# A trunk layer whose instruction order a planner writes: the heads' transposes, scores and values placed further behind their operands except for the last heads, and selects counted longer

## The chip, the core and the metric

The kernel runs on one core of a Trainium2 chip. The core has TensorE (PE, with its weight loads shown apart as PEld), VectorE (DVE), ScalarE (ACT), GpSimd (POOL) and a queue that issues DMAs (SP). Each engine works through its own list of instructions in the order in which the program was built, and waits on semaphores for the others. The metric is the device time of one execution in microseconds, the median of several runs; lower is better. Before the change it is 942.58 us (three runs, 942.47 to 942.61).

## What is computed

One layer over 512 tokens of 2048 channels, all in float32:

```
h    = rms_norm(x, norm_g)
proj = h @ w_in                  # 2048 x 8192: qA kA vA gA | qB kB vB gB
# A: 8 heads of 128, stick-breaking attention, strictly causal
z = qA @ kA.T * scale
log_stay = where(causal, log_sigmoid(-z), 0)
after = reversed_cumsum(log_stay) - log_stay
w = where(causal, exp(log_sigmoid(z) + after), 0);  ya = w @ vA
# B: 8 heads of 128, rms-normed q and k, bias by distance, softmax
scores = qB @ kB.T * scale + bias;  yb = softmax(scores) @ vB
out = x + concat(ya * silu(gA), yb * silu(gB)) @ w_out
```

## The kernel before

**The products.** The input projection is cut into 32 units of 256 output channels, in groups of four (query, key, value, gate of two heads); four further units are the output projection. A unit takes four steps, each with 512 KB of weights, and most units use a Winograd scheme of seven block products per step. To keep float32 accuracy every product is three matmuls (`three`, L530 to L532): high part by high part, low by high, high by low. The high part of the weights is a cast on ACT (`wh`, L384), the low part a difference on DVE (`wl`, L388); both are double buffered, and a cast into a buffer waits until PE has used it up.

**The heads.** While PE works on the products of later units, the heads of finished groups are handled piecewise in between. For an A head, `score` issues the score matmuls of four query blocks (b = 0 to 3; three matmuls each, into one of three spare banks); `score_a` then runs Abs, Exp and Ln on ACT (L967 to L969), a causal select on POOL (L962), Relu on ACT (L971), a second select, a scan (L974) and a subtraction (L977) on DVE, which frees the bank, a third select, and an Exp on ACT (L980). `turn` transposes the weights on PE (L1107) and splits them (L1115, L1116). `v_turn` transposes the values (L1138), scales them on ACT (L1144) and splits them; `values` multiplies them. B heads go through `prep_b` (two more transposes, L1008) and `score_b` instead, where a softmax on ACT ends in L1091. Heads are numbered 0 to 15; heads 0, 1, 4, 5, 8, 9, 12 and 13 are A heads.

**What sets the order.** A planner runs while the program is built. Every piece of work is a generator that yields an `Op` with an engine and a duration that the planner counts for it (`DV`, `AC`, `G` for POOL, `M` for PE). The planner keeps a clock of its own; when an engine is free by that clock, it takes from the engine's ready list the operation that is due first. An operation comes onto the ready list some time after its predecessor's planned end (`wait` in `advance`, L174): 0.4 us for PE, 0.06 us for the others. PE's own list goes first, and with nothing on it PE gets the next block of products (`next_product`), which is two triples of matmuls in units 2 to 31. So the numbers decide only where an instruction stands in the list of its engine; on the chip each waits for its real operands.

`position[0]` counts the blocks of products issued so far, and `at_step[step_of[NU - 4, 0]]` is the first block of unit 28, the first of the last group.

Of the kernel before, what the change touches and what calls it, by code (L numbers as in the profile page):

```python
# [26 lines left out]
NEG_BIG = -1e30  # L27
# [5 lines left out]
NU = 4 * NG  # L33
# [30 lines left out]
def trunk_kernel(ctx: ExitStack, tc: tile.TileContext, xT, xn, wi, wqk, wo, ng, qg, kg, rel, out):  # L64
# [34 lines left out]
    def tmp(shape, tag, name, dt=F32, bufs=1):  # L99
        return wp.tile(shape, dt, tag=tag, name=name, bufs=bufs)  # L100
# [33 lines left out]
    def later(t, fn):  # L134
        count[0] += 1
        heapq.heappush(events, (t, count[0], fn))
# [12 lines left out]
    def DV(w, fn, due=None, n=1):  # L149
        return Op("DVE", (0.075 + 1.04e-3 * w) * n, fn, due)  # L150

    def AC(w, fn, due=None, n=1):
        return Op("ACT", (0.085 + 0.85e-3 * w) * n, fn, due)

    def STT(w, fn, due=None):
        return Op("DVE", 0.13 + 1.04e-3 * w, fn, due)

    def M(cost, fn):
        return Op("PE", cost, fn, 0.0)

    def G(cost, fn, due=None):
        return Op("POOL", cost, fn, due)
# [5 lines left out]
    def advance(gen, rank):  # L168
        r = next(gen, None)
        if r is None:  # L170
            return
        if isinstance(r, Op):

            wait = 0.4 if r.engine == "PE" else 0.06  # L174
            later(clock[0] + wait, lambda: ready[r.engine].append((r, gen, rank, count[0])))
        else:
            waiting.append((rank, r, gen))

    def spawn(gen, rank=(0,)):
        advance(gen, rank)  # L180
# [10 lines left out]
    def schedule(next_product):  # L191

        while True:
            while True:

                go_on = False
                for w in sorted(waiting, key=lambda w: w[0]):
                    if w in waiting and w[1]():
                        waiting.remove(w)
                        advance(w[2], w[0])  # L200
                        go_on = True
                if not go_on:
                    break
            for e in ready:
                if busy[e] > clock[0] + 1e-9:
                    continue
                if ready[e]:
                    k = min(ready[e], key=lambda k: (k[0].due(), k[3]))
                    if clock[0] < held[e] - 1e-9 and k[0].due() > clock[0] + 1.5:
                        continue  # L210
                    ready[e].remove(k)
                    op, gen, rank, _ = k
                    end = issue(e, op)
                    later(end, lambda gen=gen, rank=rank: advance(gen, rank))
                    later(busy[e], lambda: None)
                    if op.hold:
                        held[e] = busy[e] + 0.2
                        later(held[e], lambda: None)
                elif e == "PE":
                    op = next_product()  # L220
                    if op is not None:
                        later(issue(e, op), op.after)
                        later(busy[e], lambda: None)
# [30 lines left out]
    at_step = {}  # L254
# [47 lines left out]
    step_of = {s_: n for n, s_ in enumerate(steps_)}  # L302
# [6 lines left out]
    position = [0]  # L309
# [240 lines left out]
    for k in reversed(range(len(program))):  # L550
        n, x, a = program[k]
# [337 lines left out]
    def take(who):  # L889

        yield lambda: len(owner) < len(SPARE)
        i = next(i for i in SPARE if i not in owner)
        owner[i] = who
        return i

    def give(i):
        del owner[i]
# [8 lines left out]
    def drop(tag, i):  # L906
        live[tag][i] = False

    def head(g, h):
        return 2 * g + h  # L910
# [29 lines left out]
    def score(g, h):  # L940

        n = head(g, h)
        yield lambda: all(("prep", n, k) in done for k in range(2)) and (n == 0 or ("scores", n - 1) in done)
        for b in range(NT):
            i = None
            if g % 2 == 0:
                i, = yield from buffer("L")
            else:
                yield lambda: n in bias
            k, = yield from buffer("W")  # L950
            z_ = yield from take(("score", n, b))
            w = P * (b + 1)
            L = tmp([P, S], "L", "L")[:, :w] if g % 2 == 0 else None
            W = tmp([P, S], "W", "W", bufs=3)[:, :w]
            yield M(0.05 + 0.35 * max(256, w) / 256, lambda: scores(banks[:, z_, :], n, b))
            z = banks[:, z_, :w]
            spawn(score_a(n, b, z_, z, L, W, w, i, k) if g % 2 == 0 else score_b(n, b, z_, z, W, w, k), (n, 1))
        done.add(("scores", n))

    def causal(x, fill):  # L960

        pool.affine_select(out=x, in_=x, compare_op=ALU.is_gt, fill=fill, base=0, pattern=[[-1, P]], channel_multiplier=1)  # L962

    def score_a(n, b, z_, z, L, W, w, i, k):
        d = slice(w - P, w)
        q_ = rstds[:, b:b + 1]
        yield AC(w, lambda: act.activation(L, z, AF.Abs, scale=q_))  # L967
        yield AC(w, lambda: act.activation(L, L, AF.Exp, scale=-1.0))
        yield AC(w, lambda: act.activation(L, L, AF.Ln, bias=1.0))  # L969
        spawn(causal_log(n, b, L[:, d]), (n, 1))  # L970
        yield AC(w, lambda: act.activation(W, z, AF.Relu, scale=q_))  # L971
        yield G(0.35, lambda: causal(W[:, d], 0.0))
        yield lambda: ("log", n, b) in done
        yield Op("DVE", 0.08 + 2.1e-3 * w, lambda: dve.tensor_tensor_scan(  # L974
            out=W[:, ::-1], data0=L[:, ::-1], data1=W[:, ::-1], initial=0.0, op0=ALU.add, op1=ALU.add))
        drop("L", i)
        yield STT(w, lambda: dve.scalar_tensor_tensor(out=W, in0=z, scalar=q_, in1=W, op0=ALU.mult, op1=ALU.subtract))  # L977
        give(z_)
        yield G(0.35, lambda: causal(W[:, d], NEG_BIG))
        yield AC(w, lambda: act.activation(W, W, AF.Exp))  # L980
        spawn(turn(n, b, W, k), (n, 2))

    def causal_log(n, b, x):
        yield G(0.35, lambda: causal(x, 0.0))
        done.add(("log", n, b))


# [107 lines left out]
    def turn(n, b, src, k):  # L1095

        yield lambda: ("turn", n, b - 1) in done if b else ("values", n - 1) in done if n else all(("staged", j, 0) in done for j in range(NJ))
        i = yield from take(("turn", n, b))
        if b == 0:
            wT[n] = [tmp([P, 13, P], x, x, F32R) for x in ("wth", "wtl")]  # L1100
            spawn(zeros(n), (n, 2))
        th, tl = wT[n]
        t = banks[:, i, :]

        def fn():
            for j in range(b + 1):
                pe.transpose(t[:, j * P:(j + 1) * P], src[:, j * P:(j + 1) * P], ident)  # L1107

        yield M(0.13 * (b + 1), fn)
        done.add(("turn", n, b))  # L1110
        drop("W", k)
        w = (b + 1) * P
        tv = t[:, :w].rearrange("p (a c) -> p a c", c=P)
        blocks = slice(b, b + 3 * b + 1, 3)
        yield AC(w, lambda: act.copy(th[:, blocks, :], tv))  # L1115
        yield DV(w, lambda: dve.tensor_tensor(out=tl[:, blocks, :], in0=tv, in1=th[:, blocks, :].bitcast(F32), op=ALU.subtract))  # L1116
        give(i)
        done.add(("turned", n, b))
# [9 lines left out]
    def v_turn(g, h):  # L1128
        n = head(g, h)
        yield lambda: "R" in done and ("unit", 4 * g + 2) in done  # L1130
        yield lambda: ("values", n - 1) in done if n else all(("staged", j, 0) in done for j in range(NJ))
        i = yield from take(("v", g, h))
        f = C[g, 2][:, h, :]
        b = banks[:, i, :]

        def fn():
            for t in range(NT):
                pe.transpose(b[:, t * P:(t + 1) * P], f[:, t * P:(t + 1) * P], ident)  # L1138

        yield M(0.5, fn)  # L1140

        def scaled():
            for t in range(NT):
                act.activation(f[:, t * P:(t + 1) * P], b[:, t * P:(t + 1) * P], AF.Copy, scale=rstd[:, t:t + 1])  # L1144

        yield Op("ACT", 0.8, scaled)
        give(i)
        d = vv[n] = tmp([P, 2, S], "v", "v", F32R)
        yield AC(512, lambda: act.copy(d[:, 0, :], f))
        yield DV(512, lambda: dve.tensor_tensor(out=d[:, 1, :], in0=f, in1=d[:, 0, :].bitcast(F32), op=ALU.subtract))  # L1150
        done.add(("v read", n))
        done.add(("v", g, h))
# [134 lines left out]
```

## Time and profile before

| | |
|---|---|
| median of three runs | 942.58 us |
| the profiled execution's own time | 941.64 us |
| its span, from the first instruction to the last | 939.9 us |
| mean granted TensorE clock | 0.998 |
| issued matmuls | 7344 |
| selects on POOL (L962) | 96, 63.8 us busy |

The span is 1.7 us shorter than the execution's own time, and the execution 0.9 us shorter than the median of the runs. In the views, "idle before" is time for which an engine did nothing ahead of an instruction, with the instruction that ended it. PEld is the loading of a matmul's stationary operand, which runs ahead of the matmul while the one before still streams.

### The profile page before, as it was taken

To read this page: it belongs to the slowest core of one execution; us is meant where nothing else is said; L and a number is where in the kernel's file an instruction comes from. 1 tells how busy PE (TensorE), PEld (TensorE's weight loads), DVE (VectorE), ACT (ScalarE), POOL (GpSimd) and SP (SyncE) were. 2 spreads that over 40 slices of the span, in tenths; PEclk is the share of its full clock that TensorE was granted. 3 is DMA by queue.
4 is the path that set the end of the run, shared out by engine and by line. 5 is a ranking of instruction groups with operands and counts; after the bars stand their busy time and mean duration, and the time that the engine had idled before them with its cause. 6 is when DMAs were issued, how large, how long until landed. Compare 5 with 4: busy or idle time off the path is not lost.

```text
span 939.9 us, 19289 instructions
## 1 busy us (share of the span) xinstructions
PE 925.2 (98%) x7344; PEld 903.5 (96%) x7344; DVE 826.1 (88%) x1562; ACT 604.2 (64%) x1150; POOL 82.2 (9%) x157
## 2 busy tenths in 40 slices
PE   9999999999999999999999999999999999999997
PEld 6899999999999999999999999999999999999997
DVE  8999998988898989888989898889989988778785
ACT  7776876884578557845785588457759785534332
POOL 0001220000122000001220000002300000101010
PEclk9999999999999999999999999999999999999999
DMA  8762223233322332233223322332222445556371
GB/s 271 237 208 91 92 91 100 82 105 105 104 91 79 120 106 82 92 110 112 85 78 122 112 80 90 113 111 74 97 91 90 147 153 182 141 199 191 112 191 45
DMA packets 63916, 112.41 MB, mean 120 GB/s; under 512 B 7248, under 2 KB 11856, under 8 KB 63824
## 3 DMA queue, kind: packets, MB, share of 16 engines
q1 hardware_dynamic: 61680, 107.51, 35.1%
q0 software_dynamic: 1728, 3.15, 2.0%
q8 instruction: 57, 0.93, 0.4%
q10 hardware_dynamic: 416, 0.52, 0.2%
q14 instruction: 35, 0.29, 0.1%
HBM read 102.77 MB, written 8.39 MB: 118 GB/s over the span
## 4 chain that ended last, share of the span: by engine, by line
PE 59%; issue 27%; DVE 7%; ACT 3%; POOL 2%; DMA 1%; POOLq 0%; SPq 0%; DVEq 0%; ACTq 0%
PE banks L530 19%; PE banks L531 18%; PE banks L532 18%; DVE wl L388 2%; POOL W L962 2%; PE banks L1107 1%; PE banks L1008 1%; DMA wt<-in_wi 1%; ACT wh L384 1%; DVE W L977 1%; DVE U L722 0%; DVE W L974 0%; DVE wt L362 0%; ACT c L1144 0%; PE banks L1138 0%
## 5 line engine op out<-in xcount | busy, mean ns | idle before, releaser
L530 PE MATMUL banks<-xh,wh 128*128 128x256 f32 (+1 forms) x1744 | 508.1, 291 | 0.1
L532 PE MATMUL banks<-xh,wl 128*128 128x256 f32 (+1 forms) x1744 | 500.3, 287 | 0.3 <-DVE wl L388 0.2
L531 PE MATMUL banks<-xl,wh 128*128 128x256 f32 (+1 forms) x1744 | 500.0, 287 | 0.0
L384 ACT CAST wh<-wt 128x1024 fp32r<-128x1024 f32 (+3 forms) x308 | 286.5, 938 | 237.3 <-PE banks L531 144.0
L388 DVE TENSOR_TENSOR wl<-wt,wh 128x768 fp32r<-128x768 f32 (+3 forms) x308 | 332.4, 1081 | 67.8 <-ACT wh L384 64.6
L530 PEld LDWEIGHTS banks<-xh,wh 128*128 128x128 f32 x1744 | 334.0, 192 | 4.2 <-ACT xh L520 0.7
L532 PEld LDWEIGHTS banks<-xh,wl 128*128 128x128 f32 x1744 | 333.6, 191 | 4.0 <-DVE wl L388 1.6
L531 PEld LDWEIGHTS banks<-xl,wh 128*128 128x128 f32 x1744 | 333.9, 191 | 3.3 <-DVE xl L521 0.3
L531 PE MATMUL banks<-wl,xh 128*128 128x256 f32 x432 | 122.3, 283 | 0.0
L532 PE MATMUL banks<-wh,xl 128*128 128x256 f32 x432 | 122.3, 283 | 0.0
L530 PE MATMUL banks<-wh,xh 128*128 128x256 f32 x432 | 122.2, 283 | 0.0
L362 DVE TENSOR_TENSOR wt<-wt 128x512 f32<-128x512 f32 x144 | 99.4, 690 | 6.1 <-DMA wt<-in_wo 4.8
L530 PEld LDWEIGHTS banks<-wh,xh 128*128 128x128 f32 x432 | 82.9, 192 | 0.0
L531 PEld LDWEIGHTS banks<-wl,xh 128*128 128x128 f32 x432 | 82.9, 192 | 0.0
L532 PEld LDWEIGHTS banks<-wh,xl 128*128 128x128 f32 x432 | 82.9, 192 | 0.0
L366 DVE TENSOR_TENSOR wt<-wt 128x256 f32<-128x256 f32 x144 | 60.5, 420 | 2.5
L365 DVE TENSOR_TENSOR wt<-wt 128x256 f32<-128x256 f32 x144 | 60.6, 421 | 2.1
L962 POOL TENSOR_SCALAR_AFFINE_SELECT W<-W 128x128 f32<-128x128 f32 x64 | 44.1, 689 | 94.5 <-DVE W L977 74.9
L962 POOL TENSOR_SCALAR_AFFINE_SELECT L<-L 128x128 f32<-128x128 f32 x32 | 19.7, 615 | 284.7 <-ACT L L969 278.1
L705 ACT COPY U<-banks 128x512 f32<-128x512 f32 x36 | 21.0, 584 | 25.0 <-PE banks L532 25.0
L1107 PE MATMUL banks<-ident,W 128*128 128x128 f32 x160 | 29.2, 281 | 3.8 <-ACT W L1091 2.4
L1116 DVE TENSOR_TENSOR wtl<-banks,wth 128x128 fp32r<-128x128 f32 (+1 forms) x64 | 30.9, 482 | 0.3 <-ACT wth L1115 0.2
(166 smaller groups left out, 1023.6 us busy)
## 6 DMA issues: line engine op xcount, KB each, us to landing
wt<-in_wi SPq DMA_DIRECT2D x254, 256.0 KB, 2.9
wt<-in_wo SPq DMA_DIRECT2D x64, 256.0 KB, 3.2
xs<-in_xn SPq DMA_DIRECT2D x16, 256.0 KB, 4.1
mixd<-c SPq DMA_DIRECT2D x16, 256.0 KB, 2.0
out<-co SPq DMA_DIRECT2D x16, 256.0 KB, 6.0
x<-in_xT SPq DMA_DIRECT2D x14, 256.0 KB, 4.3
co<-in_xn POOLq DMA_DIRECT2D x12, 256.0 KB, 6.3
bias<-in_rel SPq DMA_DIRECT2D x8, 256.0 KB, 3.4
```

The source lines that it names most:

```text
L362: yield DV(512, lambda: dve.tensor_tensor(out=some(t, 8, -7, 2), in0=some(t, 5, -5, 2), in1=some(t, 1, 0, 2), op=ALU.add), need(k0, 4))
L365: yield DV(256, lambda: dve.tensor_tensor(out=some(t, 9, 2), in0=some(t, 8, 2), in1=some(t, 0, 2), op=ALU.add), need(k1, 4))
L366: yield DV(256, lambda: dve.tensor_tensor(out=some(t, 12, 1), in0=some(t, 9, 2), in1=some(t, 4, 2), op=ALU.add), need(k1, 3.5))
L384: act.copy(whl[n, part][0][:, c], t)
L388: yield DV(c.stop - c.start, lambda: dve.tensor_tensor(out=l[:, c], in0=t, in1=h[:, c].bitcast(F32), op=ALU.subtract), need(k, 0.5))
L530: pe.matmul(o, lh, rh, start=start, stop=False, **kw)
L531: pe.matmul(o, lh, rl, start=False, stop=False, **kw)
L532: pe.matmul(o, ll, rh, start=False, stop=stop, **kw)
L705: act.copy(x[0], pair(u, a, 0, 1))
L962: pool.affine_select(out=x, in_=x, compare_op=ALU.is_gt, fill=fill, base=0, pattern=[[-1, P]], channel_multiplier=1)
L1107: pe.transpose(t[:, j * P:(j + 1) * P], src[:, j * P:(j + 1) * P], ident)
L1116: yield DV(w, lambda: dve.tensor_tensor(out=tl[:, blocks, :], in0=tv, in1=th[:, blocks, :].bitcast(F32), op=ALU.subtract))
```

## The change

The wait of 0.4 us for PE becomes 1.4 us as long as the planner has not reached unit 28, and stays 0.4 us from there on. It holds for every PE operation that a generator yields: transposes, scores and values. Products are not affected directly, as they come from `next_product`. A select is counted with 0.6 us instead of 0.35 us, and the scaling of the values in `v_turn` with 1.25 us instead of 0.8 us. No instruction is added or removed.

```diff
         if isinstance(r, Op):
-            wait = 0.4 if r.engine == "PE" else 0.06
+            wait = 0.06 if r.engine != "PE" else 1.4 if position[0] < at_step[step_of[NU - 4, 0]] else 0.4
             later(clock[0] + wait, lambda: ready[r.engine].append((r, gen, rank, count[0])))
...
-        yield G(0.35, lambda: causal(W[:, d], 0.0))
+        yield G(0.6, lambda: causal(W[:, d], 0.0))
...
-        yield G(0.35, lambda: causal(W[:, d], NEG_BIG))
+        yield G(0.6, lambda: causal(W[:, d], NEG_BIG))
...
-        yield G(0.35, lambda: causal(x, 0.0))
+        yield G(0.6, lambda: causal(x, 0.0))
...
-        yield Op("ACT", 0.8, scaled)
+        yield Op("ACT", 1.25, scaled)
```

What this does to the lists of the engines is shown at three places.

**PE, head 4: from the score of its first block to that block's transpose.** `qk4` are the split queries and keys of the head, `xh` and `wh` the split activations and weights of the products, `W` the block's attention weights. Before:

```order
L530 MATMUL banks_80<-qk4_2859 128x256
L531 MATMUL banks_80<-qk4_2859 128x256
L532 MATMUL banks_80<-qk4_2859 128x256
...
L530 MATMUL banks_80<-xh5_238,wh0_42_3074 128x256
L531 MATMUL banks_80<-xl5_239,wh0_42_3074 128x256
L532 MATMUL banks_80<-xh5_238,wl0_42_3075 128x256
L1107 MATMUL banks_80<-ident_68,W_3141 128x128
```

The same place in the changed kernel:

```order
L530 MATMUL banks_80<-qk4_2818 128x256
L531 MATMUL banks_80<-qk4_2818 128x256
L532 MATMUL banks_80<-qk4_2818 128x256
...
L530 MATMUL banks_80<-xh7_348,wh0_43_3136 128x256
L531 MATMUL banks_80<-xl7_349,wh0_43_3136 128x256
L532 MATMUL banks_80<-xh7_348,wl0_43_3137 128x256
L1107 MATMUL banks_80<-ident_68,W_3140 128x128
```

Before, 45 matmuls of products lie between the score and the transpose; now 63 do, and the transpose stands in weight step 43 instead of 42.

**PE, head 1: from the transpose of its last block to its values.** `wth` and `wtl` are the split transposed attention weights, `v` the split values. Before:

```order
L1107 MATMUL banks_80<-ident_68,W_1638 128x128 x4
L530 MATMUL banks_80<-xh0_118,wh0_24_1704 128x256
...
L531 MATMUL banks_80<-xl1_122,wh1_24_1731 128x256
L532 MATMUL banks_80<-xh1_121,wl1_24_1732 128x256
L530 MATMUL banks_80<-wth_1555,v_1627 128x512
```

In the changed kernel:

```order
L1107 MATMUL banks_80<-ident_68,W_1712 128x128 x4
L530 MATMUL banks_80<-xh4_203,wh0_26_1822 128x256
...
L532 MATMUL banks_80<-xh5_238,wl1_26_1851 128x256
L1008 MATMUL banks_80<-ident_68,c5_1764 128x128 x4
L530 MATMUL banks_80<-wth_1573,v_1642 128x512
```

Before, 24 matmuls of products lie between; now 30 do, and four transposes of the next head besides. The whole place has moved from step 24 to step 26.

**ACT, head 5: its second block.** The 128x128 rows are block 0, the 128x256 rows block 1; `wh` is a cast of product weights. Before:

```order
L967 ACTIVATE L_3553<-banks_80,rstds_76 128x256
L980 ACTIVATE W_3499<-W_3499 128x128
L968 ACTIVATE L_3553<-L_3553 128x256
L384 CAST wh1_48_3580<-wt48_3394 128x768
L969 ACTIVATE L_3553<-L_3553 128x256
L971 ACTIVATE W_3554<-banks_80,rstds_76 128x256
```

In the changed kernel:

```order
L980 ACTIVATE W_3539<-W_3539 128x128
L967 ACTIVATE L_3621<-banks_80,rstds_76 128x256
L968 ACTIVATE L_3621<-L_3621 128x256
L969 ACTIVATE L_3621<-L_3621 128x256
L971 ACTIVATE W_3622<-banks_80,rstds_76 128x256
L384 CAST wh0_50_3694<-wt50_3522 128x1024
```

The Exp of block 0 (L980), which waits for a select on POOL, and a cast of weights stood inside the chain of block 1; now the one stands ahead of it and the other behind it.

The last 1455 rows of PE, from the middle of head 15 to the end of the program, read alike in both kernels.

## Prediction

> **What bounds the kernel now.** I read the page first, then TensorE instruction by instruction, then the waits of its weight loads.
>
> ```profile
> span 939.9 us, 19289 instructions
> PE 925.2 (98%) x7344; PEld 903.5 (96%) x7344; DVE 826.1 (88%) x1562; ACT 604.2 (64%) x1150; POOL 82.2 (9%) x157
> PEclk9999999999999999999999999999999999999999
> ```
>
> PE is busy nearly all the time and its granted clock is full in every slice, so the end is set by how many matmuls there are, at which cadence, and by what PE loses between them. The change leaves the matmuls alone; it can only touch the losses. How a loss looks is seen at the first transpose of head 7, in the timeline of PE and of its loads (start, length, what):
>
> ```profile
> 381.31 0.28 PE L531 MATMUL banks<-xl,wh 128*128 128x256 f32 x1
> 381.43 0.28 PE L532 MATMUL banks<-xh,wl 128*128 128x256 f32 x1
> 382.19 0.33 PE L1107 MATMUL banks<-ident,W 128*128 128x128 f32 x1 [0.48 <-ACT W L1091]
> ...
> 382.19 0.14 PEld L1107 LDWEIGHTS banks<-ident,W 128*128 128x128 f32 x1 [0.69 <-ACT W L1091]
> ```
>
> Products start every 0.12 us. Here 0.76 us pass between two starts, so 0.64 us are lost, although the matmul row counts 0.48 us idle (its matmuls are drawn 0.28 us long, more than twice the cadence). The row of the load says 0.69, close to the true loss. I therefore add up the waits of the loads, over the whole span (total us, times, longest):
>
> ```profile
> PEld banks L1107 <- ACT W L1091: 4.3, 9, 0.7
> PEld banks L1107 <- ACT W L980: 2.8, 8, 0.4
> PEld banks L530 <- DVE W L977: 2.7, 3, 0.9
> PEld banks L530 <- DVE wtl L1116: 1.0, 1, 1.0
> PEld banks L1107 <- ACT c L1144: 0.5, 2, 0.3
> PEld banks L1107 <- DVE wtl L1116: 0.4, 2, 0.2
> PEld banks L530 <- DVE st L1083: 0.3, 1, 0.3
> PEld banks L1138 <- DVE R L880: 0.3, 1, 0.3
> PEld banks L531 <- DVE qk L929: 0.3, 1, 0.3
> PEld banks L532 <- DVE v L1150: 0.3, 1, 0.3
> PEld banks L530 <- DVE qk L1056: 0.2, 1, 0.2
> PEld banks L531 <- DVE wtl L1116: 0.2, 1, 0.2
> ```
>
> All twelve rows are work of the heads: 31 waits, **13.3 us** together, 1.4% of the span. That is the most that the change can win by them. The loads of products wait for a split of weights three times, the last time at 12.89 us, before the change begins:
>
> ```profile
> PEld banks L532 <- DVE wl L388: 1.6, 3, 0.6
> 12.89 0.19 PEld L532 LDWEIGHTS banks<-xh,wl 128*128 128x128 f32 x1 [0.64 <-DVE wl L388]
> ```
>
> The Trainium skill ("Perfetto Trace Analysis", Identifying the Most-Contended Engine) says the same of the two rows: a matmul's busy time is a poor measure because matmuls are pipelined, and the loads are the better one. By the matmuls' own waits the prize would be 2.4 + 2.1 + 0.8 + 0.6 = 5.9 us instead of 13.3; the starts at 381.43 and 382.19 decide for the loads.
>
> ```profile
> PE banks L1107 <- ACT W L1091: 2.4, 6, 0.5
> PE banks L530 <- DVE W L977: 2.1, 3, 0.7
> PE banks L530 <- DVE wtl L1116: 0.8, 1, 0.8
> PE banks L1107 <- ACT W L980: 0.6, 4, 0.2
> ```
>
> **The change part by part.** *The 1.4 us.* A transpose, score or values becomes eligible 1.0 us later in the plan; as products come in blocks of six matmuls, 6 x 0.12 = 0.72 us, most are put one to three blocks further behind the work that makes their operands. The real wait shrinks by the added distance if the operands do not come later themselves. I counted PE's list of both kernels at the 0.12 us cadence for every wait in the rows above.
>
> - B heads, L1091, 4.3 us: of the nine transposes seven stand 0.7 to 4.0 us further behind their scores. Two stand no further: block 3 of head 2, the longest with 0.7, and block 2 of head 3, with 0.17:
>
> ```profile
> 196.11 0.20 PEld L1107 LDWEIGHTS banks<-ident,W 128*128 128x128 f32 x2 [0.17 <-ACT W L1091]
> ```
>
>   Gone: 4.3 - 0.7 - 0.2 = 3.4.
> - A heads, L980, 2.8 us, 0.35 each: four stand about 2.2 us further (head 4 is the place shown: 18 matmuls more, 2.16 us), 1.4 gone; block 3 of heads 4, 8 and 12 stands only 0.28 further, 0.84 gone; the first block of head 0 no further. Gone: 2.2.
> - Values of head 1, L1116, 1.0 us: 6 matmuls (0.72 us) and four transposes more, which take this long elsewhere (start, length in the chain that ended last):
>
> ```profile
> 316.94 0.44 PE banks L1008 x4
> ```
>
>   So 1.16 us more against a wait of 1.0: gone. Of the other 0.6 us on L1116 I count half. Gone: 1.3.
> - L1144 (0.5) and L880 (0.3): 4 and 0.7 us further, gone. Of the four rows left (st, qk twice, v; 1.1 us), half: 0.55. Gone: 1.35.
>
> *The selects at 0.6 us.* The scores that wait for L977 wait for a bank, which the second block's subtraction frees. ACT and the places where it ends, head 5:
>
> ```profile
> 280.80 0.47 ACT L967 ACTIVATE L<-banks,rstds 128x256 f32<-128x256 f32 x1
> 282.29 0.31 ACT L980 ACTIVATE W<-W 128x128 f32<-128x128 f32 x1 [1.01 <-POOL W L962]
> ...
> 282.81 0.82 ACT L384 CAST wh<-wt 128x768 fp32r<-128x768 f32 x1
> 283.54 0.41 ACT L969 ACTIVATE L<-L 128x256 f32<-128x256 f32 x1
> ...
> 286.43 0.48 DVE L977 SCALAR_TENSOR_TENSOR W<-banks,rstds,W 128x256 f32<-128x256 f32 x1
> ...
> 286.96 0.44 PE L530 MATMUL banks<-qk 128*128 128x384 f32 x1 [0.68 <-DVE W L977]
> ```
>
> Between Abs (L967) and Ln (L969) of block 1, ACT stood 1.01 us for a select and then did L980 and a cast of 0.82 us. Both leave this chain now, about 2 us, and the next score stands 0.7 us further behind. In head 13 only the cast leaves, enough with the 0.7. All three waits go: 2.7. The cast moved behind four short activations comes some 1.5 us later; what covers it is that ACT is ahead of PE by far more:
>
> ```profile
> ACT wh L384 <- PE banks L531: 144.0, 118, 3.7
> ```
>
> ACT waits 118 times until PE lets go of a weight buffer, 1.2 us on average. Without that cover a late cast costs PE its own length, 0.94 us (mean of L384, below).
>
> *The values' scaling at 1.25 us* moves its split later on DVE, and so the values; it takes 18.1 / 16 = 1.13 us a head, so the plan is nearer to the chip. I give it nothing of its own.
>
> ```profile
> L1144 ACT ACTIVATE c<-banks,rstd 128x128 f32<-128x128 f32 x64 | 18.1, 367 | 0.2 <-PE banks L1138 0.2
> L384 ACT CAST wh<-wt 128x1024 fp32r<-128x1024 f32 (+3 forms) x308 | 286.5, 938 | 237.3 <-PE banks L531 144.0
> ```
>
> *What is new.* Nearly every helper of 16 heads stands elsewhere, so some that found their operand ready may not now. The trace cannot show these; the bounds are none at all and the 10.95 us just counted. Heads 4 to 15 repeat one pattern three times (L977: three waits, all alike), so I take one new wait per repeat, of the mean size of the first row, 4.3 / 9 = 0.48: 1.4 us.
>
> *The end.* From unit 28 on the wait is 0.4 as before, and PE's last 1455 rows are the same, so the output projection starts no later in the list. The stores and loads that feed it go through SP's and POOL's queues in nearly the same order; I count them at nothing, hidden behind the products of the last units. If that cover were gone, the place would be PE's first rows of the output projection.
>
> **Sum:** 3.4 + 2.2 + 2.7 + 1.3 + 1.35 - 1.4 = 9.55, say **9.5 us** less. The profiled execution took 941.64 us (its span and 1.7 around it) and would take 932.1; the median of the runs is 0.94 higher, 942.58, so I predict **933.1**.
>
> **The rivals.** *Everything goes and nothing new comes*: 942.58 - 13.3 = 929.3. For it speaks that no wait is longer than the added 1.0 us; against it, that three places do not move.
>
> *A select has no fixed length.*
>
> ```profile
> L962 POOL TENSOR_SCALAR_AFFINE_SELECT W<-W 128x128 f32<-128x128 f32 x64 | 44.1, 689 | 94.5 <-DVE W L977 74.9
> 280.88 1.21 DVE L388 TENSOR_TENSOR wl<-wt,wh 128x1024 fp32r<-128x1024 f32 x1
> 281.04 1.22 POOL L962 TENSOR_SCALAR_AFFINE_SELECT W<-W 128x128 f32<-128x128 f32 x1 [1.10 <-DVE W L977]
> ```
>
> The mean is 0.689, over the 0.6 now counted, and beside a DVE split of 1.21 us one took 1.22. In the new order the selects meet other DVE work; if they are late as often as before, the A heads keep their 2.2 + 2.7, the gain is 4.6 and the time 938.0. The Trainium skill ("SBUF — State Buffer") speaks for this rival: DVE work with two SBUF inputs and GpSimd share a port pair that is locked for a whole instruction, so a select would stand still rather than slow down; the row at 281.04 agrees.
>
> *The waits travel along*: the helpers stand later, but their operands too, because ACT's and DVE's lists moved with them; 942.6. Against it: the distances counted above are those from score to transpose, and they grew.
>
> *Slower.* Four ACT pieces of a head now run in one go ahead of a cast, so weights come late at a unit's steps and PE waits for `wl`. A late cast costs 0.94 us; from ten such steps of the 128 before the output projection the gain is used up, and with 14 the time is 933.1 + 14 x 0.94 = 946.3. Against it: the 144 us above, and no product wait after 12.89 us.
>
> **How the numbers follow.** My forecast (930.5 to 936.5) gets 0.58, everything gone 0.10, the selects 0.18 (936.5 to 940.7), waits travelling along 0.09, slower 0.05. A measurement can tell 0.2%, 1.9 us, from no change: faster 0.86, same 0.09, slower 0.05. The range, 929.8 to 938.5, holds the forecast, half of the better case and most of the selects: 0.79.
>
> **What would show it.** The waits of PE's loads should sum to some 4 us for the heads instead of 13.3: no row for L977, L1091 with at most four waits, L980 about 0.6, no 1.0 on L1116. ACT's waits for selects should shrink:
>
> ```profile
> ACT W L980 <- POOL W L962: 20.7, 22, 3.1
> ```
>
>  My forecast is wrong if PE's loads wait for `wl` or `wh` after that, if rows of the same total stand under other releasers, or if the span after unit 28 grows.

## The result, and the profile after

The changed kernel takes **929.34 us** (median of four runs, 929.16 to 929.42) against 942.6 us before (942.47 to 942.79): ratio 0.9859, 95% interval 0.9842 to 0.9876. That is 13.3 us less, where 9.5 were predicted, and 0.5 us below the range that was given. Run again later, the same pair gave 929.02 against 942.02 us, ratio 0.9866 (0.9851 to 0.9880). One execution is left out of everything below: 2297.28 us for the kernel with a select counted 0.75 us, whose other three took 929.23 to 929.59.

The page of the changed kernel, its span and busy times:

```profile
span 927.7 us, 19258 instructions
PE 919.2 (99%) x7344; PEld 902.9 (97%) x7344; DVE 823.0 (89%) x1562; ACT 601.5 (65%) x1147; POOL 79.6 (9%) x157
```

The matmuls are the same 7344. The span is 12.2 us shorter and the loads' busy time has hardly moved (903.5 to 902.9): what went is time between the loads, 36.4 us before (939.9 - 903.5) and 24.8 now. These are the waits of PE's loads for work of the heads, all that the view still lists (total us, times, longest):

```profile
PEld banks L1107 <- ACT W L980: 0.6, 2, 0.3
PEld banks L1107 <- ACT W L1091: 0.4, 1, 0.4
PEld banks L1107 <- DVE st L1083: 0.3, 1, 0.3
PEld banks L530 <- DVE W L977: 0.2, 1, 0.2
PEld banks L530 <- DVE wtl L1116: 0.2, 1, 0.2
```

Twelve rows with 31 waits and 13.3 us have become five with six waits and 1.7 us. The 11.6 us that disappeared equal the fall in the loads' idle time and are nearly the whole of the 12.2. ACT waits less for selects too, although the selects of `W` are not shorter on average (0.689 us before):

```profile
ACT W L980 <- POOL W L962: 12.9, 10, 2.3
...
L962 POOL TENSOR_SCALAR_AFFINE_SELECT W<-W 128x128 f32<-128x128 f32 x64 | 45.8, 716 | 95.3 <-DVE W L977 83.0
```

### The profile page after: what moved, and what is told of

Same layout as the page of the kernel before. It is cut to its first block, busy times and chain, and to the rows that moved or that the text cites. A ratio compares the mean times of both kernels' runs of the same rounds, so it can differ in the third digit from the quotient of the medians.

```text
span 927.7 us, 19258 instructions
## 1 busy us (share of the span) xinstructions
PE 919.2 (99%) x7344; PEld 902.9 (97%) x7344; DVE 823.0 (89%) x1562; ACT 601.5 (65%) x1147; POOL 79.6 (9%) x157
## 4 chain that ended last, share of the span: by engine, by line
PE 96%; DVE 1%; ACT 1%; issue 1%; DMA 0%; POOL 0%; SPq 0%; DVEq 0%
PE banks L530 31%; PE banks L531 31%; PE banks L532 31%; PE banks L1107 2%; PE banks L1008 1%; PE banks L1138 1%; DMA x<-in_xT 0%; ACT wh L384 0%; DVE wl L388 0%; DVE xt L474 0%; DVE wt L362 0%; ACT W L1089 0%; DVE co L723 0%; ACT W L1082 0%; ACT c L1144 0%
## 5 line engine op out<-in xcount | busy, mean ns | idle before, releaser
L388 DVE TENSOR_TENSOR wl<-wt,wh 128x1024 fp32r<-128x1024 f32 (+3 forms) x308 | 333.3, 1085 | 52.5 <-ACT wh L384 50.7
L962 POOL TENSOR_SCALAR_AFFINE_SELECT L<-L 128x128 f32<-128x128 f32 x32 | 14.8, 463 | 276.9 <-ACT L L969 275.2
L1116 DVE TENSOR_TENSOR wtl<-banks,wth 128x128 fp32r<-128x128 f32 (+1 forms) x64 | 30.9, 483 | 0.7 <-issue 0.4
L1115 ACT CAST wth<-banks 128x128 fp32r<-128x128 f32 (+1 forms) x64 | 27.2, 425 | 5.8 <-PE banks L1107 5.8
```

The costliest lines, as they stand in the source:

```text
L388: yield DV(c.stop - c.start, lambda: dve.tensor_tensor(out=l[:, c], in0=t, in1=h[:, c].bitcast(F32), op=ALU.subtract), need(k, 0.5))
```

## The experiments

Times stand beside 941.8 to 942.0 us for the kernel before on the same chip in the same hour, and beside 929.02 us for the changed kernel, run again on one of these chips.

### The parts alone

```diff
-            wait = 0.4 if r.engine == "PE" else 0.06
+            wait = 0.06 if r.engine != "PE" else 1.4 if position[0] < at_step[step_of[NU - 4, 0]] else 0.4
```

> Only the wait of 1.4 us; selects and value scaling counted as before. Theory 1 (each part removes the waits of PE's loads that the prediction gave it): the three waits for the subtraction L977 stay, 2.7 us, the other 10.6 go; time about 932. Theory 2 (the more exact durations do most of it, because they put ACT's work into an order in which nothing stands behind a select): 937 to 940, with most of the waits for L980 and L977 still there.

Measured: 935.42 us, ratio 0.9928 (0.9912 to 0.9945): 6.4 us of the gain. Neither theory holds. There is no wait for L977 any more, which the first theory kept, and the waits for L980 are more than twice those of before. The loads, and around the longest of these waits POOL, ACT and PE:

```profile
PEld banks L1107 <- ACT W L980: 6.9, 11, 1.6
...
451.49 2.96 POOL L962 TENSOR_SCALAR_AFFINE_SELECT W<-W 128x128 f32<-128x128 f32 x1 [2.02 <-DVE W L977]
...
454.48 0.52 ACT L980 ACTIVATE W<-W 128x384 f32<-128x384 f32 x1 [2.59 <-POOL W L962]
...
455.06 0.33 PE L1107 MATMUL banks<-ident,W 128*128 128x128 f32 x1 [1.36 <-ACT W L980]
```

One select lasted 2.96 us where the plan counts 0.35; 1.0 us more of distance does not cover that.

```diff
-        yield G(0.35, lambda: causal(W[:, d], 0.0))
+        yield G(0.6, lambda: causal(W[:, d], 0.0))
...
-        yield Op("ACT", 0.8, scaled)
+        yield Op("ACT", 1.25, scaled)
```

> Only the durations (select 0.6, value scaling 1.25); PE's wait stays 0.4 us. Theory 1: the 2.7 us of L977 go and at most half of L980's 2.8; the waits for L1091 (4.3) stay; time 938 to 940. Theory 2: about 932.

Measured: 937.42 us, ratio 0.9954 (0.9939 to 0.9969): 4.4 us. A little under the first theory's times, far from the second's. The L977 waits are gone here too, and half of the B heads' waits, which the durations were not expected to touch:

```profile
PEld banks L1107 <- ACT W L980: 3.0, 8, 0.5
PEld banks L1107 <- ACT W L1091: 2.0, 4, 0.7
```

Apart the parts give 6.4 and 4.4 us, together 13.0: some 2.2 us come only when both are there. The runs of the wait alone spread from 934.43 to 936.49 us, so this difference is known to about 1 us.

### Where the last half microsecond comes from

> The kernel before, unchanged, with a profile of another execution. If the 0.94 us between the profiled execution and the median was the profile of one lucky execution, this one's own time is 942.5 and its waits of PE's loads sum to about 1 us more than 13.3. If a profiled execution is always 0.9 us shorter than others of this kernel, it is again 941.6 with the same rows.

Measured: 941.78 us beside a median of 941.82, span 940.1, and the same rows of waits (4.4, 2.8 and 2.7 us for L1091, L980 and L977).

> The changed kernel, unchanged, beside the kernel before on one chip. If the 0.94 us between the profiled execution and the median of before belonged to the chip or the hour (another execution with a profile had 941.8 beside a median of 941.82), the gain here is the difference of the profiled spans, 12.2 us, and the ratio 0.987. If it is a loss in unprofiled executions, the gain is again 13.3 us and the ratio 0.9859.

Measured: 929.02 against 942.02 us, ratio 0.9866 (0.9851 to 0.9880), span 927.0. So a profiled execution of the kernel before is not shorter than others as a rule. Its executions spread from 941.65 to 942.57 us within one later series on one chip, so the 0.94 us that the prediction added is no more than they differ by anyway; whether the chip or the hour has a part in it is not shown. The profiled spans differ by 12.2 us in the first pair, the medians by 13.3 there and by 13.0 in this one; the gain is known to about half a microsecond.

### How far the numbers may be moved

```diff
-            wait = 0.06 if r.engine != "PE" else 1.4 if position[0] < at_step[step_of[NU - 4, 0]] else 0.4
+            wait = 0.06 if r.engine != "PE" else 1.4
```

> The changed kernel, but 1.4 us for the last heads too. Theory A (the exemption is needed: the last heads have nothing behind them to hide in): heads 14 and 15 end some us later, the output projection waits for them, 1 to 4 us slower than the changed kernel. Theory B (there is room there too): the waits after unit 28 (some 1.3 us) go, 928 to 929.

Measured: 933.32 us, ratio 0.9909 (0.9895 to 0.9924); theory A, though 4.3 us slower than the changed kernel are a little more than it allowed. The waits that theory B names did go: the view lists no transpose any more. But two waits at the end of the heads make up what is lost, of the last values for their weights and of an output product for its activations:

```profile
PEld banks L530 <- DVE wtl L1116: 2.6, 1, 2.6
PEld banks L530 <- ACT xbwth L520: 1.9, 1, 1.9
```

Behind the last heads comes the output projection, which needs their result; here distance is time.

The next three change one number of the changed kernel each, `else 1.4 if` to 0.9, to 1.1 and to 2.4.

> The changed kernel with a wait of 0.9 instead of 1.4 us. If the durations do the larger part and the wait only has to cover what is left, the waits of PE's loads are under 3 us and the time 929 to 931. If the wait must cover the largest lateness, about 1 us beyond the old 0.4, some 4 us of waits come back: 932 to 934.

> The changed kernel with a wait of 1.1 us. If the result is flat around the chosen numbers (0.9 gave 929.6, a select of 0.75 gave 929.4), 929 to 930.5. If each order is a draw of its own, anywhere between 929 and 936.

> The changed kernel with a wait of 2.4 instead of 1.4 us. If only the waits of PE's loads count, nothing is left to gain and the time is 929 to 930. If later helpers cost something (buffers held longer, the last heads pushed against the output projection), product loads wait from about 600 us on and the time is 931 to 935.

Measured: 929.64, 930.59 and 932.79 us (ratios 0.9870, 0.9879 and 0.9908, the last 0.9893 to 0.9922). Half the added wait is enough with the longer durations, and 2.4 us lose 3.8, though product loads do not wait from 600 us on, as was expected: at 166 and 170 us PE's products wait for DVE to empty a unit's bank. The largest row is another, and 1.64 of its 1.9 us stand behind a select of 3.63 us. The loads, and the split of weights that stood on DVE ahead of the second bank's L723:

```profile
PEld banks L1107 <- ACT W L980: 1.9, 2, 1.6
...
PEld banks L530 <- DVE c L723: 1.4, 1, 1.4
PEld banks L530 <- DVE c L712: 1.3, 1, 1.3
...
169.37 1.22 DVE L388 TENSOR_TENSOR wl<-wt,wh 128x1024 fp32r<-128x1024 f32 x1 [0.91 <-ACT wh L384]
```

So head work pushed later can meet the end of a unit on DVE, and late selects return. No load of a product waits for its own weights there, but the second bank wait has a late cast in it: DVE stood 0.91 us for a cast (which had itself waited for PE), did the split, and only then emptied the bank.

```diff
-        yield Op("ACT", 1.25, scaled)
+        yield Op("ACT", 1.05, scaled)
```

> The changed kernel with the value scaling counted 1.05 us instead of 1.25. Theory C (the count matters because it comes near the true 1.1 us): as good as the change, 929 to 930. Theory D (each set of numbers gives another order, and in some a select meets a run of DVE work by chance): anywhere between 929 and 936, without relation to how near the number is.

Measured: 930.66 us, ratio 0.9885 (0.9868 to 0.9902), with single runs from 929.25 to 932.81. That is outside theory C's range, although 1.05 is nearer to the measured 1.13 us than 1.25 is. The order's one long wait of a transpose, 1.60 us at 315.97 us, stands behind this select, as theory D has it:

```profile
311.63 3.62 POOL L962 TENSOR_SCALAR_AFFINE_SELECT W<-W 128x128 f32<-128x128 f32 x1 [5.33 <-DVE W L977]
```

And the changed kernel with `G(0.75, ...)` in place of `G(0.6, ...)`:

> The changed kernel with a select counted 0.75 us instead of 0.6, nearer to the measured mean of 0.69. Theory C (nearer counts are better): 928.5 to 929.5. Theory D (another draw): anywhere between 929 and 936; the waits of PE's loads for L980 say which.

Measured: 929.27 us (the middle of three), ratio 0.9867 (0.9850 to 0.9883). There is no trace of these three, so the waits for L980 that were to tell the theories apart are not known. The four neighbours (waits of 0.9 and 1.1, scaling 1.05, select 0.75) lie within 1.7 us of the change, with overlapping intervals: around the chosen numbers the result is nearly flat, and none of them beats it.

### The value scaling

```diff
-        yield Op("ACT", 1.25, scaled)
+        yield Op("ACT", 0.8, scaled)
```

> The changed kernel with the value scaling counted 0.8 us again (wait 1.4, select 0.6). Theory S (the scaling, 1.1 us on ACT, stood inside the B heads' chains because it was counted short, and its count took it out): waits for L1091 and L1144 return, some 1 to 2 us, time about 931. Theory N (as in the prediction, it is worth nothing of its own): 929.3 within 0.5.

Measured: 935.19 us, ratio 0.9933 (0.9918 to 0.9947). One number, to which the prediction gave nothing, decides over 6.2 us. But the waits that come back are not those of theory S: L1091 has 0.7 us and L980 has 6.3, with two of 2 us each at the same place of two repeats. There, POOL, DVE beside it, ACT and PE:

```profile
302.10 3.10 POOL L962 TENSOR_SCALAR_AFFINE_SELECT W<-W 128x128 f32<-128x128 f32 x1 [3.42 <-DVE W L977]
...
302.50 0.94 DVE L388 TENSOR_TENSOR wl<-wt,wh 128x768 fp32r<-128x768 f32 x1
303.36 0.41 DVE L365 TENSOR_TENSOR wt<-wt 128x256 f32<-128x256 f32 x1
303.70 0.68 DVE L362 TENSOR_TENSOR wt<-wt 128x512 f32<-128x512 f32 x1
304.30 0.41 DVE L366 TENSOR_TENSOR wt<-wt 128x256 f32<-128x256 f32 x1
304.64 0.41 DVE L365 TENSOR_TENSOR wt<-wt 128x256 f32<-128x256 f32 x1
...
305.23 0.52 ACT L980 ACTIVATE W<-W 128x384 f32<-128x384 f32 x1 [4.10 <-POOL W L962]
...
305.81 0.44 PE L1107 MATMUL banks<-ident,W 128*128 128x128 f32 x2 [1.86 <-ACT W L980]
```

The select starts at 302.10, and ends at 305.20, 0.15 us after the run of DVE work does (304.64 + 0.41 = 305.05).

### Without the selects

```diff
 def causal(x, fill):
-    pool.affine_select(out=x, in_=x, compare_op=ALU.is_gt, fill=fill, base=0, pattern=[[-1, P]], channel_multiplier=1)
+    pass
```

The plan still counts them, so each kernel keeps its order.

> The kernel of wait 1.4 and select 0.6 with the value scaling counted 0.8 us, with the selects left out on POOL (the causal masks are not applied), the plan unchanged. Theory P: its 6 us over the changed kernel are selects of 3 us that ACT and then PE wait for; without them 927 to 929.5. Theory R (the scaling's own place in ACT's list is late): the waits of PE for L980 stay, 934 to 935.

> The kernel with the wait of 1.4 us alone (durations as before), with the selects left out on POOL. If what it lacks against the changed kernel are late selects, the waits for L980 (6.9 us) vanish and the time is 928.5 to 930. If its order is bad in itself, 933 to 935.

> The kernel before with the selects left out on POOL (the causal masks are not applied), the plan unchanged. If the waits of the A heads (L980 and L977, 5.5 us) are the selects' length, 936 to 937. If they are mostly the place in PE's list, and the selects only the last link, 940 to 942.

Measured: 928.81, 928.76 and 936.29 us (ratio 0.9939, 0.9924 to 0.9954, for the last). Without selects the two kernels that lost 6 us are as good as the changed one: late selects alone spoiled their orders. The changed kernel itself was not run without selects; its rows leave 0.8 us on L980 and L977 that it could still gain so. In the order of before, 5.6 us go, and the loads say which:

```profile
PEld banks L1107 <- ACT W L1091: 4.3, 9, 0.7
...
PEld banks L530 <- DVE W L977: 0.5, 3, 0.2
...
PEld banks L1107 <- ACT W L980: 0.4, 1, 0.4
```

L977 fell from 2.7 to 0.5 and L980 from 2.8 to 0.4, while the B heads' 4.3 us stayed. So about two fifths of the gain (5.6 of 13.0 us) can be had by taking the selects out of the order of before, 4.6 of it in these two rows. None of the selects of before is longer than 1.5 us; those over 2 us appear only in the kernels with a raised wait.

### A select beside DVE

Three small programs put selects of 128x128 beside chosen DVE work.

> Not the layer: four stages of 8 selects of 128x128 on POOL (the output is not computed), beside nothing, beside 24 back-to-back DVE additions of two SBUF operands, beside 24 with one operand in PSUM, beside 24 copies of float32. Theory P (a select cannot start or go on while DVE holds the port they share): 0.29 us each beside nothing; beside the additions of two SBUF operands the first select takes as long as several additions, over 2 us, or all wait for a gap; beside PSUM operands or copies less or nothing. Theory Q (long selects are an error of the records, POOL's spans being rough): 0.3 to 0.7 in all four stages.

Eight selects in each row (start, time of all eight), beside nothing, additions of two SBUF operands, additions with one operand in PSUM, and copies:

```profile
2.01 2.02 POOL L115 TENSOR_SCALAR_AFFINE_SELECT a<-a 128x128 f32<-128x128 f32 x8
...
4.05 5.36 POOL L115 TENSOR_SCALAR_AFFINE_SELECT a<-a 128x128 f32<-128x128 f32 x8
...
21.82 2.02 POOL L115 TENSOR_SCALAR_AFFINE_SELECT a<-a 128x128 f32<-128x128 f32 x8
...
39.57 3.53 POOL L115 TENSOR_SCALAR_AFFINE_SELECT a<-a 128x128 f32<-128x128 f32 x8
```

That is 0.25, 0.67, 0.25 and 0.44 us a select. Two operands in SBUF hold it up, one in PSUM does not; theory Q is out, and theory P's "several additions" too: each select waits for about one.

> Not the layer: 8 selects on POOL beside nothing, beside 24 of the weight sums L362 (strided, two SBUF operands), beside 24 splits L388 of 1024 columns, and beside 24 in the layer's mix of sums and splits (the output is not computed). If a select gets its turn after each DVE instruction, it lasts one of them: 0.7, 1.2 and about 0.7 us. If in some sequences it gets no turn between two, single selects last 2 to 4 us, in the mix above all.

Measured: 5.45 / 8 = 0.68 us beside the sums, 9.19 / 8 = 1.15 beside the splits, 6.16 / 8 = 0.77 in the mix, with the longest single one 1.39 us. Again one DVE instruction each.

> Not the layer: 8 times a subtraction on DVE (one operand in PSUM), a select on POOL of its result, and seven DVE instructions behind it without a pause; these are the layer's mix of sums and splits, the sums L362, the splits of 1024 columns, and additions with an operand in PSUM (the output is not computed). If the wait for DVE's result is what lets the following run shut the select out, selects last 2 to 5 us in the first three stages, about the whole run. If a select always gets its turn after one instruction, 0.7 to 1.4 us, and what stretches it in the layer stays open. In the last stage 0.3 us.

One select in the mix, one beside the sums, one beside the splits, one beside operands in PSUM:

```profile
6.79 1.21 POOL L115 TENSOR_SCALAR_AFFINE_SELECT a<-a 128x128 f32<-128x128 f32 x1 [4.79 <-DVE a L152]
...
53.91 0.68 POOL L115 TENSOR_SCALAR_AFFINE_SELECT a<-a 128x128 f32<-128x128 f32 x1 [4.47 <-DVE a L152]
...
99.40 1.22 POOL L115 TENSOR_SCALAR_AFFINE_SELECT a<-a 128x128 f32<-128x128 f32 x1 [7.68 <-DVE a L152]
...
162.14 0.29 POOL L115 TENSOR_SCALAR_AFFINE_SELECT a<-a 128x128 f32<-128x128 f32 x1 [8.09 <-DVE a L152]
```

The select lasts as long as the one DVE instruction that stands beside it, 1.21, 0.68 or 1.22 us; over all 24 of the first three stages it is 0.42 to 1.22 us. A select of the layer that lasts through five of them did not come about here.

The rows narrow down what such a select waits for. In the twelve traces of the layer with selects in it, 660 selects last over 0.4 us, and every one of them ends 0.15 to 0.16 us after the end of a DVE row, as do the 59 of the small programs. Before that the 660 outlast 172 ends of DVE rows, and behind each of these the next DVE row starts at least 0.07 us ahead of the end: the instructions stand back to back. No select outlasts an end behind which DVE pauses, if only by 0.03 us, and 22 of the 23 selects over 1.6 us end at such a pause. The longest select of the changed kernel with the DVE rows at its end, and the DVE rows beside the first select of the mix above:

```profile
121.50 3.36 POOL L962 TENSOR_SCALAR_AFFINE_SELECT W<-W 128x128 f32<-128x128 f32 x1 [2.62 <-DVE W L977]
...
124.28 0.42 DVE L365 TENSOR_TENSOR wt<-wt 128x256 f32<-128x256 f32 x1
124.74 0.42 DVE L366 TENSOR_TENSOR wt<-wt 128x256 f32<-128x256 f32 x1
...
6.63 1.21 DVE L139 TENSOR_TENSOR wl<-t,wh 128x1024 fp32r<-128x1024 f32 x1
7.88 0.69 DVE L133 TENSOR_TENSOR t<-t 128x512 f32<-128x512 f32 x1
```

DVE pauses from 124.70 to 124.74, and the select ends at 124.86; in the small program it pauses from 7.84 to 7.88, and the select ends at 8.00. DVE pauses so behind 295 of 368 additions, sums, splits and copies of the small programs, but only behind 355 of 1278 in the changed kernel. That would be why the small programs showed no long select; it is read from the rows, as none with a long unbroken run on DVE was made. It also stays open why a select is let in at some ends without a pause (371 of the 660) and not at the 172.

## Why the prediction was right and where it was wrong

**Right: the mechanism and the row.** The end is PE's list plus what PE loses between loads. The loads' waits fell by 11.6 us and the span by 12.2; the matmul row's own waits (5.9 us) could not have held that.

**Right: the rows that should vanish.** L1116's 1.0 us, L1144, L880 and the three long waits for L977 are gone. Products still wait for `wl` only three times, the last at 13.12 us. The end came out as nothing, as counted: the last 1455 rows of PE take 175.3 us before and 175.4 after. The rival that helpers' operands travel along is out.

**Wrong in size: what stays.** The sum kept 2.3 us of old waits and charged 1.4 us for new ones, 3.7 together; 1.7 are there in all, at these loads:

```profile
88.42 0.14 PEld L1107 LDWEIGHTS banks<-ident,W 128*128 128x128 f32 x1 [0.25 <-ACT W L980]
...
128.68 0.19 PEld L530 LDWEIGHTS banks<-qk 128*128 128x128 f32 x1 [0.24 <-DVE W L977]
...
630.76 0.20 PEld L1107 LDWEIGHTS banks<-ident,W 128*128 128x128 f32 x2 [0.33 <-ACT W L980]
...
652.48 0.19 PEld L530 LDWEIGHTS banks<-wth,v 128*128 128x128 f32 x1 [0.18 <-DVE wtl L1116]
...
702.67 0.14 PEld L1107 LDWEIGHTS banks<-ident,W 128*128 128x128 f32 x1 [0.41 <-ACT W L1091]
...
746.17 0.31 PEld L1107 LDWEIGHTS banks<-ident,W 128*128 128x128 f32 x3 [0.26 <-DVE st L1083]
```

Two of them stand where a wait stood before, the first block of head 0 (88.42) and the values of head 12 (652.48): 0.4 us, where the sum kept 2.3. The other four are new, 1.2 us against the 1.4 charged, though not one to each repeat: between 129 and 630 us there is none. So the term that was mis-sized is the old waits that were kept. That L980 stands at the 0.6 that was named is partly luck, as half of it is new (the second block of head 12, at 630.76).

The step that failed is the reading of the distances: "the real wait shrinks by the added distance if the operands do not come later themselves". Where the prediction kept most, they came earlier. Block 3 of head 2, to which the prediction left its 0.7 us because it stands no further behind its score, shows it: its score, the Exp and the scaling that the transpose waits for, before and then in the changed kernel:

```profile
166.55 0.49 PE L530 MATMUL banks<-qk 128*128 128x512 f32 x1
174.16 0.81 ACT L1089 ACTIVATE W<-W,st,yn 128x512 f32<-128x512 f32 x1
176.34 0.74 ACT L1091 ACTIVATE W<-W,st 128x512 f32<-128x512 f32 x1
```

```profile
180.83 0.40 PE L530 MATMUL banks<-qk 128*128 128x512 f32 x1
185.80 0.82 ACT L1089 ACTIVATE W<-W,st,yn 128x512 f32<-128x512 f32 x1 [0.38 <-DVE st L1088]
188.45 0.76 ACT L1091 ACTIVATE W<-W,st 128x512 f32<-128x512 f32 x1
```

From score to the end of L1091 the chain took 10.5 us and takes 8.4, because other work stands on ACT ahead of its Exp (L1089), which started 7.6 us after the score and starts 5.0 after it. In block 2 of head 3, the other place that stands no further, 8.1 us became 6.6. Elsewhere the chain grew and the distance grew more: in block 3 of head 7 it took 8.8 us and takes 10.1, but the transposes start 11.3 us after the score instead of 8.9. Distance on PE was counted and the length of the chain was not. These two places are 0.9 us of the 2.3. The rest, among it the halves that were kept without a count, came to 0.4 instead of 1.4; of each of these the reason stays open. Head 5, where the prediction did look at ACT's list, came out as it said: Abs to Ln of block 1 took 280.80 to 283.54 and takes 283.58 to 284.52.

```profile
283.58 0.46 ACT L967 ACTIVATE L<-banks,rstds 128x256 f32<-128x256 f32 x1
...
284.52 0.42 ACT L969 ACTIVATE L<-L 128x256 f32<-128x256 f32 x1
```

**Wrong: the parts as separate terms.** The 2.7 us of L977 were put down to the selects' count; either part alone removes them. "I give it nothing of its own", for the value scaling, misses by 6.2 us: not because the scaling was late, but because its count is one of the numbers that decide which DVE work stands beside which select. Without selects the 0.8 us cost nothing (928.81).

**The level, in part chance.** The prediction took its gain off the median, 0.94 us above the profiled execution, and single executions of the kernel before differ by that much. Of the 3.8 us between 933.1 and 929.34, about 2.0 are the waits above and 0.6 the loads' busy time; 1.1 are what the first pair of medians lies wider apart (13.3 us) than its profiled spans (12.2), and those are not explained.

**The rivals.** "Everything goes and nothing new comes" gave 929.3 and met the time, though not quite its mechanism: 1.7 us of waits are left, 1.2 of them new, and the 0.6 us of busy time and the 1.1 us of the level happen to make up for them. To meet the time so closely is luck. It had a chance of 0.10, and the range stopped just above it. The rival of the selects names a real mechanism, worth 5.6 us in the order of before, and it decides the kernel with the wait alone and the one with the scaling at 0.8 us; for the durations alone it was not tested. It lost here because the changed order keeps its long selects where PE hardly waits for them. It has four over 2 us, and no transpose waits after the longest, the one at 121.50 shown above. The slower rival's sign, a product's load that waits for its weights after the first 14 us, appeared in no trace of these orders; a late cast showed only indirectly, in one bank wait with the wait of 2.4 us.

## What to carry to other kernels

Where a planner's order is executed against real semaphores, read the loss from the waits of the bottleneck's loads, and find from the trace how late each chain really is: here a margin of half that size to that size, with durations near those of the trace, recovered nearly all of it (nearer durations were no better), and a wider margin was lost again where something waited behind it. Effects of plan numbers do not add up: each number makes another order, so test the parts together, and some neighbours, before one of them is called the cause. To forecast such a change, compare the lists of the engines that make the operands, not only that of the engine that waits.

## What the runs showed of the hardware

A select of 128x128 on POOL takes 0.25 to 0.29 us beside nothing or beside DVE work with an operand in PSUM, and as long as one DVE instruction (0.4 to 1.4 us) beside work with two operands in SBUF. The Trainium skill ("SBUF — State Buffer", SBUF: two separate sides) describes this, a port pair that is locked for a whole instruction and also taken by float32 copies; the copies agree, with 0.44 us a select. It does not say when a select gets in among several DVE instructions. In the layer a select lasted up to 4.31 us and outlasted up to seven of them. By the rows, a select never outlasted an end behind which DVE paused for 0.03 us or more, and every end it did outlast was followed back to back; it ended 0.15 to 0.16 us after the end at which it was let in. This is read from the traces and was not tested by a program made for it.
